# One step of a hybrid decoder layer: dummy products ahead of the small ones, weight parts in another order, and a few moved steps

## The chip, the cores and the metric

The kernel runs on one core of one Trainium2 chip, in one launch. The metric is the device time of that launch in microseconds (us). The core has five engines that work side by side, each through its own instructions in a fixed order: PE (TensorE, matrix products; its weight loads are listed apart as PEld), DVE (VectorE), ACT (ScalarE), POOL (GpSimd) and SP (SyncE, which here issues transfers). Products are written to PSUM, everything else lives in SBUF or in the chip's memory.

## The reference, cut to what matters

Eight sampled sequences of 8 tokens and one prompt of 512 tokens go through one layer; the kernel lays all of them side by side as 576 columns, with the channels on the 128 partitions.

```python
u = rmsnorm(h, norm_mix); P = u @ w_in              # 1024 -> z, xbc, dt, and the RWKV columns rw
# group A (Mamba-2 SSD): causal conv(4) + SiLU on xbc, chunked state space recurrence, gate silu(z), grouped RMSNorm
# group B (RWKV-7): u = rw + (prev - rw) * mu; decay, in-context rate, normalised key kk;
#   S_t = S diag(w) - (S kk)(kk*a)^T + v k^T, read with r; norm per head, bonus, gate
h = h + concat(y_ssd, y_rwkv) @ w_out
h = h + (silu(hf @ w_gate) * (hf @ w_up)) @ w_down   # hf = rmsnorm(h, norm_ffn); 1024 -> 2816 -> 1024
h = h + sigmoid(rmsnorm(h, norm_ple) @ w_ple_gate) * (p @ w_ple_proj)
y = rmsnorm(h, norm_final)                           # and the new states
```

## The kernel before, in words

**Dense tiles.** Each product with a weight matrix is made tile by tile: 128 output channels by 576 columns, in PSUM. For precision every float32 operand is split in two: a rounded first part (hi) and the remainder (lo). A weight block of 128x512 (four 128x128 blocks) is transferred into `raw`, ACT rounds it to `whi` (line 195), and POOL and DVE in turn subtract to make `wlo` (line 198, the turn is kept in `flip`). `whi` and `wlo` have two buffers each. `linear` (line 217) then makes, per 128x128 block and per half of 288 columns, three products through `mm3`: whi with x-hi (line 213), whi with x-lo (214), wlo with x-hi (215). So a weight block gives 24 products, and `whi` is used by the 23rd of them, `wlo` by the 24th.

**Order.** The program is written in Python, and a scheduler that knows the dependencies places each instruction in the queue of its engine when the kernel is built. On the chip each engine then works strictly in that order, waiting for what is not ready.

**Stages.** (1) The opening: x is loaded, an unnormalised split copy `xu` feeds the first tiles (the two low-rank tiles and the six of quarter 0), while the normalised X is made (`norm_x`, line 330: one DVE multiplication and one split per 128 channels, eight in all); `gates` makes the eight gate tiles. (2) Four quarters of group B, four heads each. A quarter has `prep` (decays, keys; `by_channel` at line 489 turns per-token norms into per-channel rows by small products with the identity), `start_states` (line 706, 32 small products with the sampled start states), `gram` (line 581: nine 64-token chunks in five PSUM tiles, 72 products of 64x128, line 593, which ACT and DVE read out and POOL masks), `solve` (30 dependent steps on DVE), `combine` (line 661, 64 products of 32x32 and again 64), `chain` (line 719, nine dependent steps with `core`, `prompt_state` and `outp`) and `head_norm` (line 866). Dense tiles of the next quarter, of the convolution and of z are filled in between. (3) Group A (`ssd`). (4) The output projection: `scaled` (line 1292) adds the group A part, in two passes of eight tiles, and `after` (line 1275) prepares the next input. (5) The feed-forward part, 44 and then 8 tiles. (6) The gated per-layer embedding in two column ranges (320 and 256 columns), each with a final norm and eight stores of `yT`, all issued by SP (line 1392).

ACT needs a table load before a function that its present table does not have; square roots (`inv_norm`, `rstd_by_token`) stand among tanh, exp and sigmoid.

Of the kernel before, what the change touches and what calls it, by code (L numbers as in the profile page):

```python
# [16 lines left out]
P = 128  # L17
# [40 lines left out]


CONV_BC = [8, 9, 10, 11]  # L60
CONV_X = [0, 1, 2, 3, 4, 5, 6, 7]
# [13 lines left out]
def hybrid_step(ctx, tc, A):  # L75
# [15 lines left out]
    def act(out, in_, func=AF.Copy, scale=1.0, bias=0.0):  # L91
        S.activation(out, in_, func, bias=bias, scale=scale)  # L92

# [80 lines left out]
    wat = [0]  # L174
    flip = [0]

    def split(src, pool, tags, shape, lo_eng=None, hi=None, lo=None, hi_eng=None, **kw):
# [11 lines left out]
    def wsplit(src, n, hi=None, lo=None):  # L189
        raw = wp.tile([P, 512], F32, tag="raw", name=nm("raw"), bufs=3)  # L190
        nc.sync.dma_start(raw[:, 0:n], src)
        if hi is None:
            hi = wp.tile([P, 512], F32R, tag="whi", name=nm("whi"))
            lo = wp.tile([P, 512], F32R, tag="wlo", name=nm("wlo"))
        act(hi[:, 0:n], raw[:, 0:n])
        flip[0] += 1
        eng = G if flip[0] % 2 else V
        eng.tensor_tensor(lo[:, 0:n], raw[:, 0:n], hi[:, 0:n].bitcast(F32), ALU.subtract)  # L198
        return hi, lo
# [17 lines left out]
    def linear(xs, ps):  # L217
        nk = len(xs)
        for k in range(0, nk, 4):
            b = min(4, nk - k)  # L220
            hi, lo = wload(b)
            for i in range(b):
                xh, xl = xs[k + i]
                mm3(ps, hi[:, i * P:(i + 1) * P], lo[:, i * P:(i + 1) * P], xh, xl, k + i == 0, k + i == nk - 1)

# [19 lines left out]
    nc.sync.dma_start(sst[:], A["s_shift"])  # L245
    sho = se.tile([P, 26, 9], F32, tag="sho", name="sho")

    def cx_ps():
# [178 lines left out]

    norm_x(3)
    ugh = gate_in()
    norm_x(5)  # L430

# [57 lines left out]
    def by_channel(rn, jj, psum, tag):  # L489

        rnv = rn[:].rearrange("p (w h) -> p w h", w=5)[:, :, jj * 2:jj * 2 + 2].unsqueeze(3)
        if tag:
            rx = sp.tile([P, 5, 2, 64], F32, tag=tag, name=nm(tag), bufs=1)
            V.tensor_copy(rx[:], rnv.to_broadcast([P, 5, 2, 64]))
            rx4 = rx[:, 4]
        else:
            rx = slot("rx", [P, 4, 2, 64])
            V.tensor_copy(rx[:], rnv[:, 0:4].to_broadcast([P, 4, 2, 64]))
            rx4 = s2.tile([P, 2, 64], F32, tag="rx4", name=nm("rx4"))
            V.tensor_copy(rx4[:], rnv[:, 4].to_broadcast([P, 2, 64]))  # L500
        ps = psum()
        for w, a in enumerate(WIN[:4]):
            T.transpose(ps[:, a:a + P], rx[:, w].rearrange("p a b -> p (a b)"), ident[:])
        yield 0, 448, ps[:, 0:448]
        ps = psum()
        T.transpose(ps[:, 0:P], rx4.rearrange("p a b -> p (a b)"), ident[:])
        yield 448, NT, ps[:, 0:P]
# [73 lines left out]
    def gram(s):  # L581

        s.Lst = s2.tile([P, 9, 2, 64], F32, tag="Lst", name=nm("Lst"))
        for gs in ((0,), (1, 2), (3, 4), (5, 6), (7, 8)):
            n = len(gs)
            gl = slice(gs[0], gs[0] + n)
            mk = dgmask if gs[0] == 0 else gmask
            ps = lin.tile([P, 1024], F32, tag="lin", name=nm("lin"))
            for i, g in enumerate(gs):
                for jj in jj2:  # L590
# [70 lines left out]
    def combine(s):  # L661
# [3 lines left out]
        for e in range(2):  # L665
            for z in range(2):
# [4 lines left out]
                              s.Ad[e].rearrange("g s t -> s g t"))  # L671
        Wp = cx_ps()
        Wv = Wp[:].rearrange("p (g j t) -> p g j t", g=8, j=2)
        for g in range(1, 9):
# [5 lines left out]
        for e in range(2):  # L680
# [3 lines left out]
            else:  # L684
                V.tensor_scalar(AA[hi_:hi_ + 32, 1:9], Wv[hi_:hi_ + 32], -1.0, None, ALU.mult)
        Xp = cx_ps()
        Xv = Xp[:].rearrange("p (g j t) -> p g j t", g=8, j=2)
        for g in range(1, 9):
# [30 lines left out]
    def chain(s):  # L719
# [45 lines left out]
        def core(g):  # L765
# [21 lines left out]
        def outp(g):  # L787
            sv = suv(g)
            ow = outs[g]
            for jj in jj2:  # L790
                for e in range(2):
                    T.matmul(ow[H[e], jj], sv[:, jj, 1, e], Gt[:, g, jj, 1, e], start=False, stop=True,  # L792
                             skip_group_check=True)
            act(AR[:, :, g], ow)

# [70 lines left out]
    def head_norm(s, ahead=()):  # L866
# [18 lines left out]
        for jj in jj2:  # L885
# [10 lines left out]
            else:  # L896
                YR.append(split(y, xp, ("xhi", "xlo"), [P, NT], lo_eng=G))

# [5 lines left out]
    for s in Q:  # L904
        if s.q == 0:
            fill(2)
            gates(ugh)
        fill_for(s)
# [443 lines left out]
    for a, b in ((0, 320), (320, NT)):  # L1352
        n = b - a
        acc = None
        for c in range(8):
# [15 lines left out]
            V.tensor_tensor(t, ps, rs[:, a:b], ALU.mult)  # L1371
            act(t, t, AF.Sigmoid)
            V.tensor_tensor(t, t, PL[c][:, a:b], ALU.mult)  # L1373
# [11 lines left out]
        for c in range(8):  # L1385
# [4 lines left out]
            else:  # L1390
                V.scalar_tensor_tensor(h, h, par("norm_final", c), ps, ALU.mult, ALU.mult)
            nc.sync.dma_start(A["yT"][c, :, a:b], h)

# [131 lines left out]
```

## Time and profile before

| what | value |
|---|---|
| median of 3 runs | 1366.8 us (1364.27 to 1370.2) |
| the profiled execution's own time | 1370.43 us |
| its span, first to last instruction | 1368.7 us |
| PE busy | 1259.1 us, 10565 products |
| DVE, ACT, POOL busy | 719.6, 577.4, 550.2 us |
| mean granted TensorE clock | 0.947 of full speed |
| transfers | 135.56 MB, mean 99 GB/s |

Busy times are sums over one engine's instructions; a busy PE is not PE at its peak, since products overlap and their ends are modelled. The granted clock is the share of full speed that PE was given in a stretch. In a row of the timeline stand the start, the duration, the engine, the line, the operation, output and inputs, and in brackets how long the engine had been idle and whose result it waited for.

### The profile page before, as it was taken

To read this page: it belongs to the slowest core of one execution; us is meant where nothing else is said; L and a number is where in the kernel's file an instruction comes from. 1 tells how busy PE (TensorE), PEld (TensorE's weight loads), DVE (VectorE), ACT (ScalarE), POOL (GpSimd) and SP (SyncE) were. 2 spreads that over 40 slices of the span, in tenths; PEclk is the share of its full clock that TensorE was granted. 3 is DMA by queue.
4 is the path that set the end of the run, shared out by engine and by line. 5 is a ranking of instruction groups with operands and counts; after the bars stand their busy time and mean duration, and the time that the engine had idled before them with its cause. 6 is when DMAs were issued, how large, how long until landed. Compare 5 with 4: busy or idle time off the path is not lost.

```text
span 1368.7 us, 26325 instructions
## 1 busy us (share of the span) xinstructions
PE 1259.1 (92%) x10565; PEld 1160.4 (85%) x10565; DVE 719.6 (53%) x1333; ACT 577.4 (42%) x1148; POOL 550.2 (40%) x543
## 2 busy tenths in 40 slices
PE   6897999999989979899989979999999999999986
PEld 5786897789868857777779769999999999999985
DVE  7648766787687785843367676522222221111255
ACT  6565345634653553344425364432332332222253
POOL 5326414632454153133456676432332332334332
PEclk9997899899979989989999989999999999999998
DMA  4322342234223312362644532233232222222432
GB/s 162 124 70 62 85 119 60 81 100 128 61 90 91 101 58 84 88 209 82 189 145 142 183 97 71 70 85 79 84 85 81 83 85 77 82 80 79 148 92 69
DMA packets 94458, 135.56 MB, mean 99 GB/s; under 512 B 34704, under 2 KB 39056, under 8 KB 94336
## 3 DMA queue, kind: packets, MB, share of 16 engines
q1 hardware_dynamic: 94336, 133.88, 32.8%
q8 instruction: 83, 1.36, 0.4%
q14 instruction: 39, 0.32, 0.1%
HBM read 106.10 MB, written 27.75 MB: 98 GB/s over the span
## 4 chain that ended last, share of the span: by engine, by line
PE 60%; DVE 15%; ACT 5%; DMA 5%; issue 4%; POOL 3%; DVEq 0%; SPq 0%; ACTq 0%; POOLq 0%
PE lin L215 16%; PE lin L213 16%; PE lin L214 16%; DVE h L375 2%; DVE Tt L656 1%; DVE tmp L654 1%; DMA raw<-wts 1%; POOL wlo L198 1%; DVE suv L809 1%; PE cx L777 1%; PE lin L593 1%; PE cx L769 1%; DVE wlo L198 1%; PE cx L792 1%; DVE pg L1373 1%
## 5 line engine op out<-in xcount | busy, mean ns | idle before, releaser
L213 PE MATMUL lin<-xhi,whi 128*128 128x288 f32 (+1 forms) x1488 | 450.8, 303 | 3.3 <-ACT whi L92 2.2
L215 PE MATMUL lin<-xhi,wlo 128*128 128x288 f32 (+1 forms) x1488 | 447.9, 301 | 3.2 <-POOL wlo L198 2.2
L214 PE MATMUL lin<-xlo,whi 128*128 128x288 f32 (+1 forms) x1488 | 447.7, 301 | 1.0 <-POOL xlo L186 1.0
L198 POOL TENSOR_TENSOR wlo<-raw,whi 128x512 fp32r<-128x512 f32 x136 | 182.8, 1344 | 501.9 <-ACT whi L92 462.1
L92 ACT ACTIVATE whi<-raw 128x512 fp32r<-128x512 f32 (+1 forms) x272 | 168.8, 621 | 397.7 <-PE lin L214 341.1
L213 PEld LDWEIGHTS lin<-xhi,whi 128*128 128x128 f32 (+1 forms) x1488 | 281.4, 189 | 10.5 <-ACT whi L92 2.6
L215 PEld LDWEIGHTS lin<-xhi,wlo 128*128 128x128 f32 (+1 forms) x1488 | 282.3, 190 | 7.0 <-POOL wlo L198 2.8
L214 PEld LDWEIGHTS lin<-xlo,whi 128*128 128x128 f32 (+1 forms) x1488 | 281.9, 189 | 6.1 <-POOL xlo L186 2.1
L198 DVE TENSOR_TENSOR wlo<-raw,whi 128x512 fp32r<-128x512 f32 (+1 forms) x136 | 98.4, 724 | 167.4 <-ACT whi L92 164.8
L215 PE MATMUL lin<-ah,wlo 128*128 128x288 f32 x352 | 105.0, 298 | 0.9
L213 PE MATMUL lin<-ah,whi 128*128 128x288 f32 x352 | 104.0, 296 | 0.0
L214 PE MATMUL lin<-al,whi 128*128 128x288 f32 x352 | 103.8, 295 | 0.0
L215 PEld LDWEIGHTS lin<-ah,wlo 128*128 128x128 f32 x352 | 66.2, 188 | 3.2 <-POOL wlo L198 2.6
L214 PEld LDWEIGHTS lin<-al,whi 128*128 128x128 f32 x352 | 66.1, 188 | 0.0
L213 PEld LDWEIGHTS lin<-ah,whi 128*128 128x128 f32 x352 | 66.0, 187 | 0.0
L1332 DVE TENSOR_TENSOR sg<-lin,sg 128x576 f32<-128x576 f32 x22 | 16.7, 758 | 82.9 <-PE lin L215 81.7
L1327 DVE TENSOR_TENSOR sg<-lin,rstd 128x576 f32<-128x576 f32 x22 | 16.7, 758 | 69.3 <-PE lin L215 69.0
L654 DVE TENSOR_TENSOR tmp<-L,Tt 72x30 f32<-72x30 f32 (+14 forms) x120 | 48.9, 407 | 3.2
L656 DVE TENSOR_TENSOR Tt<-Tt,tmp 72x30 f32<-72x30 f32 (+14 forms) x120 | 46.1, 384 | 3.4
L213 PE MATMUL lin<-xu,whi 128*128 128x288 f32 x128 | 39.9, 313 | 8.5 <-ACT xu L92 6.9
L215 PE MATMUL lin<-xu,wlo 128*128 128x288 f32 x128 | 40.0, 314 | 7.3 <-DVE wlo L198 5.5
L186 POOL TENSOR_TENSOR al<-sg,ah 128x576 fp32r<-128x576 f32 x22 | 31.5, 1433 | 32.1 <-ACT ah L92 32.1
(370 smaller groups left out, 2513.6 us busy)
## 6 DMA issues: line engine op xcount, KB each, us to landing
raw<-wts SPq DMA_DIRECT2D x271, 256.0 KB, 2.6
S<-s_wkv SPq DMA_DIRECT2D x8, 512.0 KB, 5.1
hd<-s_ssm SPq DMA_DIRECT2D x8, 512.0 KB, 4.0
o_ssm_s<-hd SPq DMA_DIRECT2D x8, 512.0 KB, 2.9
xbc_d<-E SPq DMA_DIRECT2D x12, 288.0 KB, 2.1
x<-xT SPq DMA_DIRECT2D x8, 288.0 KB
gate_d<-g SPq DMA_DIRECT2D x8, 288.0 KB, 2.6
bv_d<-rw SPq DMA_DIRECT2D x8, 288.0 KB
```

What stands on the lines that cost most here:

```text
L92: S.activation(out, in_, func, bias=bias, scale=scale)
L186: eng.tensor_tensor(lo[:], src, hi[:].bitcast(F32), ALU.subtract)
L198: eng.tensor_tensor(lo[:, 0:n], raw[:, 0:n], hi[:, 0:n].bitcast(F32), ALU.subtract)
L213: T.matmul(ps[:, a:b], whi, xhi[:, a:b], start=first, stop=False)
L214: T.matmul(ps[:, a:b], whi, xlo[:, a:b], start=False, stop=False)
L215: T.matmul(ps[:, a:b], wlo, xhi[:, a:b], start=False, stop=last)
L375: V.scalar_tensor_tensor(h[:], E[:, i:i + 600], w(i), h[:], ALU.mult, ALU.add)
L593: T.matmul(ps[:, c:c + 128].rearrange("p (a t) -> p a t", a=2), s.BK[jj][H[e], g].rearrange("p a t -> p (a t)"), s.G[H[e], g, jj, :, e], s ...
L654: V.tensor_tensor(o, L[:, jx:jx + 1, jx + 1:32].to_broadcast([NB, jx, n]), Tt[:, 0:jx, jx:jx + 1].to_broadcast([NB, jx, n]), ALU.mult)
L656: V.tensor_tensor(Tt[:, 0:jx, jx + 1:32], Tt[:, 0:jx, jx + 1:32], o, ALU.subtract)
L1327: V.tensor_tensor(s_[:], ps, rs[:], ALU.mult)
L1332: V.tensor_tensor(s_[:], up, s_[:], ALU.mult)
```

## The change

Every text line below is from the difference of the two programs; the helper functions around it are the same.

- **Beats.** `beat` issues products of a constant mask with a broadcast column, 512 columns wide, into a PSUM tile that the following products overwrite. Their results are used by nothing. They stand ahead of the small products of `by_channel`, `gram` (numbers by the table `BEATS`), `combine`, `start_states` and two steps of one `chain`: 107 in all, 99 of 512 columns and 8 of 256.
- **First weight parts first.** `linear` makes the 16 products with `whi` of a weight block first, and the 8 with `wlo` after them.
- **Inputs one per tile.** `norm_x` is called for one input tile at a time between the first tiles, and `gates` moves behind the third tile of quarter 0.
- **Splits.** In `scaled` and the tiles of that stage DVE alone makes `wlo` (`only`); the last quarter's two outputs are split by DVE and not by POOL.
- **Square root tables.** `root_ready` puts a one-column square root on ACT behind a given instruction: after the last step of the last chain, and after the last sigmoid.
- **Stores.** In the second column range the stores of odd `c` are issued by ACT.

```diff
+BEATS = [(10, 2), (3, 1), (3, 1), (3, 1)]
...
+    def root_ready(ins):
+
+        with tc.issue_after(ins.ins):
+            t = cp.tile([P, 1], F32, tag="rr", name=nm("rr"), bufs=2)
+            act(t[:], eps_t[:, 2:3], AF.Sqrt)
...
-        eng = G if flip[0] % 2 else V
+        eng = only[0] or (G if flip[0] % 2 else V)
...
             hi, lo = wload(b)
+            w = [slice(i * P, i * P + P) for i in range(b)]
             for i in range(b):
-                xh, xl = xs[k + i]
-                mm3(ps, hi[:, i * P:(i + 1) * P], lo[:, i * P:(i + 1) * P], xh, xl, k + i == 0, k + i == nk - 1)
+                for c, d in HV:
+                    T.matmul(ps[:, c:d], hi[:, w[i]], xs[k + i][0][:, c:d], start=k + i == 0, stop=False)
+                    T.matmul(ps[:, c:d], hi[:, w[i]], xs[k + i][1][:, c:d], start=False, stop=False)
+            for i in range(b):
+                for c, d in HV:
+                    T.matmul(ps[:, c:d], lo[:, w[i]], xs[k + i][0][:, c:d], start=False, stop=k + i == nk - 1)
...
+    def beat(ps, n=1, w=512):
+
+        for _ in range(n):
+            T.matmul(ps[:, 0:w], gmask[:].rearrange("p a b -> p (a b)"), gmask[:, 0, 0:1].to_broadcast([P, w]),
+                     start=True, stop=True)
...
-    norm_x(3)
+    norm_x(1)
     ugh = gate_in()
-    norm_x(5)
+    norm_x(1)
...
         ps = psum()
+        beat(ps, 1)
         for w, a in enumerate(WIN[:4]):
...
             ps = lin.tile([P, 1024], F32, tag="lin", name=nm("lin"))
+            beat(ps, BEATS[s.q][bool(gs[0])])
...
         Wp = cx_ps()
+        beat(Wp, 2)
...
         Xp = cx_ps()
+        beat(Xp, 2)
...
+        beat(Zp, 2)
         for jj in jj2:
+            if jj:
+                beat(Zp[:, 256:512], 2, 256)
...
+            if q == 2 and g > 6:
+                beat(ups, 2)
...
+            out = act(AR[:, :, g], ow)
+            if q == 3 and g == 8:
+                root_ready(out)
...
-                YR.append(split(y, xp, ("xhi", "xlo"), [P, NT], lo_eng=G))
+                YR.append(split(y, xp, ("xhi", "xlo"), [P, NT], lo_eng=V))
...
-        if s.q == 0:
-            fill(2)
-            gates(ugh)
+        for i in range(6) if s.q == 0 else ():
+            fill(1)
+            norm_x(1)
+            if i == 2:
+                gates(ugh)
...
+    only[0] = V
     for c in range(8):
         scaled(c, 0)
...
+    only[0] = None
...
+            sig = act(t, t, AF.Sigmoid)
+            if a and c == 7:
+                root_ready(sig)
...
-            nc.sync.dma_start(A["yT"][c, :, a:b], h)
+            (nc.scalar if a and c % 2 else nc.sync).dma_start(A["yT"][c, :, a:b], h)
```

Three places show what the builder made of it. The first is the ACT queue in `prep` of quarter 0, around the square root of the key norms (`rn`). `whi_1159` before and `whi_1161` now is the rounding of the next dense tile's first weight block; `lo`, `pb`, `suv` and `G` are steps of the quarter, `E` and `h` of a convolution tile. Before:

```order
L92 ACTIVATE rn_1097<-cb_990 128x20
L92 ACT_TABLE_LOAD
L92 ACTIVATE lo_1118<-lin_1111,hw 128x576
L92 ACTIVATE pb_1121<-lo_1108 128x576
L92 ACTIVATE suv_1669<-tr_1666 64x4x64 x2
L92 ACTIVATE suv_1663<-tr_1666 64x4x64 x2
L92 ACTIVATE lo_1108<-lo_1108 128x576
L92 ACTIVATE G_982<-ar_981 64x9x64 x2
L92 ACTIVATE whi_1159<-raw_1157 128x512
L92 ACTIVATE E_1079<-lin_1015 128x512
```

The same place in the changed kernel:

```order
L93 ACTIVATE rn_1097<-cb_990 128x20
L93 ACTIVATE whi_1161<-raw_1159 128x512
L93 ACTIVATE E_1079<-lin_1015 128x512
L93 ACTIVATE E_1079<-lin_1015 128x8x8
L93 ACT_TABLE_LOAD
L93 ACTIVATE lo_1118<-lin_1111,hw 128x576
L93 ACTIVATE h_1087<-E_1079,hw 128x600
L93 ACTIVATE pb_1121<-lo_1108 128x576
L93 ACTIVATE suv_1699<-tr_1696 64x4x64 x2
```

The rounding of the weight block stood behind eight other ACT instructions and a table load, and now stands right behind the square root.

The second is PE in `gram` of quarter 1, at the third of its five PSUM tiles (`lin_3149` before, `lin_3195` now; `G` and `bk` are the gram's operands, the `cx` rows are steps of quarter 0's chain). Before:

```order
L777 MATMUL cx_1865<-xs_1862,TT_465 64x64 x4
L782 MATMUL cx_1870<-ar_981,suv_1834 64x64 x4
L593 MATMUL lin_3149<-G_2686,bk_2849 128x128 x2
L593 MATMUL lin_3149<-G_2686,bk_2986 128x128 x2
L593 MATMUL lin_3149<-G_2686,bk_2849 128x128 x2
L593 MATMUL lin_3149<-G_2686,bk_2986 128x128 x2
L792 MATMUL cx_1870<-G_982,suv_1834 64x64
```

In the changed kernel:

```order
L806 MATMUL cx_1895<-xs_1892,TT_435 64x64 x4
L811 MATMUL cx_1900<-ar_981,suv_1864 64x64 x4
L264 LDWEIGHTS gmask
L264 MATMUL lin_3195<-gmask 128x512
L615 MATMUL lin_3195<-G_2720,bk_2885 128x128 x2
L615 MATMUL lin_3195<-G_2720,bk_3024 128x128 x2
L615 MATMUL lin_3195<-G_2720,bk_2885 128x128 x2
L615 MATMUL lin_3195<-G_2720,bk_3024 128x128 x2
L821 MATMUL cx_1900<-G_982,suv_1864 64x64
```

One beat stands ahead of the tile's products; the products and the chain's steps around them keep their places.

The third is DVE in the opening, behind the normalisation of the last input tile (`x_220`). `rw` is the token shift of the two low-rank tiles, `xlo` the remainders of the normalised inputs, `wlo_573` before and `wlo_518` now is the remainder of a weight block. Before:

```order
L332 SCALAR_TENSOR_TENSOR x_220<-x_220,pv,rstd_263 128x576
L348 SCALAR_TENSOR_TENSOR rw_337<-sst,pv,rw_337 128x9
L349 SCALAR_TENSOR_TENSOR rw_337<-u_335,pv,rw_337 128x511
L351 SCALAR_TENSOR_TENSOR rw_337<-u_335,pv,rw_337 128x8x7
L186 TENSOR_TENSOR xlo_351<-x_200,xhi_350 128x576
L186 TENSOR_TENSOR xlo_361<-x_204,xhi_360 128x576
L348 SCALAR_TENSOR_TENSOR rw_427<-sst,pv,rw_427 128x9
L349 SCALAR_TENSOR_TENSOR rw_427<-u_425,pv,rw_427 128x511
L351 SCALAR_TENSOR_TENSOR rw_427<-u_425,pv,rw_427 128x8x7
L186 TENSOR_TENSOR xlo_442<-x_206,xhi_441 128x576
L186 TENSOR_TENSOR xlo_452<-x_216,xhi_451 128x576
L198 TENSOR_TENSOR wlo_573<-raw_570,whi_572 128x512
```

In the changed kernel:

```order
L351 SCALAR_TENSOR_TENSOR x_220<-x_220,pv,rstd_263 128x576
L367 SCALAR_TENSOR_TENSOR rw_337<-sst,pv,rw_337 128x9
L368 SCALAR_TENSOR_TENSOR rw_337<-u_335,pv,rw_337 128x511
L370 SCALAR_TENSOR_TENSOR rw_337<-u_335,pv,rw_337 128x8x7
L194 TENSOR_TENSOR xlo_351<-x_200,xhi_350 128x576
L367 SCALAR_TENSOR_TENSOR rw_417<-sst,pv,rw_417 128x9
L368 SCALAR_TENSOR_TENSOR rw_417<-u_415,pv,rw_417 128x511
L370 SCALAR_TENSOR_TENSOR rw_417<-u_415,pv,rw_417 128x8x7
L194 TENSOR_TENSOR xlo_432<-x_202,xhi_431 128x576
L206 TENSOR_TENSOR wlo_518<-raw_515,whi_517 128x512
```

All eight normalisations still stand ahead of the remainder of the weight block; two of the four `xlo` between them are gone. `wlo_573` belonged to the second weight block of its tile, `wlo_518` belongs to the first of the same tile.

More of the change, by code (lines that the diff above doesn't have):

```diff
@@ L91, in act @@
     def act(out, in_, func=AF.Copy, scale=1.0, bias=0.0):
-        S.activation(out, in_, func, bias=bias, scale=scale)
+        return S.activation(out, in_, func, bias=bias, scale=scale)
+    def root_ready(ins):
+        with tc.issue_after(ins.ins):
+            t = cp.tile([P, 1], F32, tag="rr", name=nm("rr"), bufs=2)
+            act(t[:], eps_t[:, 2:3], AF.Sqrt)
     lins, turn = [lin], [0]
@@ L175, in hybrid_step @@
     flip = [0]
+    only = [None]
     def split(src, pool, tags, shape, lo_eng=None, hi=None, lo=None, hi_eng=None, **kw):
@@ L505, in by_channel @@
         ps = psum()
+        beat(ps, 1)
         T.transpose(ps[:, 0:P], rx4.rearrange("p a b -> p (a b)"), ident[:])
@@ L793, in outp @@
                              skip_group_check=True)
-            act(AR[:, :, g], ow)
+            out = act(AR[:, :, g], ow)
+            if q == 3 and g == 8:
+                root_ready(out)
         def prompt_state(g):
@@ L1371, in hybrid_step @@
             V.tensor_tensor(t, ps, rs[:, a:b], ALU.mult)
-            act(t, t, AF.Sigmoid)
+            sig = act(t, t, AF.Sigmoid)
+            if a and c == 7:
+                root_ready(sig)
             V.tensor_tensor(t, t, PL[c][:, a:b], ALU.mult)
```

## The prediction

> **What bounds the kernel now.** I read the engine shares and the chain of waits on the page, then busy times by stretch. From the page, busy time and share of each engine, and the shares of the chain that ended last:
>
> ```profile
> PE 1259.1 (92%) x10565; PEld 1160.4 (85%) x10565; DVE 719.6 (53%) x1333; ACT 577.4 (42%) x1148; POOL 550.2 (40%) x543
> ...
> PE 60%; DVE 15%; ACT 5%; DMA 5%; issue 4%; POOL 3%; DVEq 0%; SPq 0%; ACTq 0%; POOLq 0%
> ```
>
> PE is busy for 92% but only 60% of the chain is its work; the rest of its busy time lies beside something else that ends later. The windows (stretch, length, busy time and count of PE, PEld, DVE, ACT and POOL, granted clock, DMA share, GB/s) separate the two kinds of stage:
>
> ```profile
> 99.00:697.00 598.00, 540.78 (x5010) 465.25 (x5011) 414.82 (x862) 282.33 (x625) 234.50 (x271) 0.91 0.34 101
> 870.00:1300.00 430.00, 429.05 (x3209) 426.42 (x3208) 93.72 (x134) 128.16 (x202) 143.56 (x106) 1.00 0.31 87
> 386.00:406.00 20.00, 17.04 (x161) 13.87 (x161) 15.60 (x32) 10.66 (x27) 6.21 (x11) 0.50 0.29 97
> 408.00:420.00 12.00, 11.27 (x119) 9.29 (x116) 4.96 (x14) 5.99 (x18) 11.54 (x12) 1.00 0.36 76
> 858.26:864.00 5.74, 5.06 (x24) 4.83 (x25) 5.49 (x4) 1.35 (x2) 4.64 (x3) 0.70 0.32 91
> ```
>
> From 870 to 1300 us, the feed-forward part, PE has no idle time and full clock; nothing in the change touches this, so 430 us stand fixed. From 99 to 697 us, the quarters, PE is busy 90% at a mean clock of 0.91, with DVE at 69%. The change works there and at the edges of stages. What the clock does to a dense product is seen in PE's timeline at a stage's start:
>
> ```profile
> 99.13 0.41 PE L213 MATMUL lin<-xhi,whi 128*128 128x288 f32 x1 [1.69 <-ACT whi L92]
> ...
> 102.20 0.44 PE L215 MATMUL lin<-xhi,wlo 128*128 128x288 f32 x1
> 102.44 0.44 PE L213 MATMUL lin<-xhi,whi 128*128 128x288 f32 x1
> ...
> 103.01 0.30 PE L213 MATMUL lin<-xhi,whi 128*128 128x288 f32 x1
> 103.14 0.30 PE L214 MATMUL lin<-xlo,whi 128*128 128x288 f32 x1
> ...
> 107.11 0.40 PE L215 MATMUL lin<-xhi,wlo 128*128 128x288 f32 x1 [0.82 <-POOL wlo L198]
> ...
> 235.36 0.40 PE L215 MATMUL lin<-xhi,wlo 128*128 128x288 f32 x1 [1.10 <-POOL wlo L198]
> ```
>
> Starts are 0.24 us apart up to 102.4 and 0.13 (0.133 over longer runs) from 103.0: half the clock doubles a dense product. I work against the profiled execution: 1370.43 us, of it 1368.7 span, 3.6 above the median of 1366.8. A result within 0.5% (6.8 us) is no change here, about what a measurement of this kernel can tell, as its runs spread over 0.43%.
>
> **Weight parts first, and the queue of ACT (T1).** The block that PE waits for at 99.13 stood behind this on ACT:
>
> ```profile
> 97.07 1.36 ACT L92 ACTIVATE G<-ar 64x576 f32<-64x576 f32 x2
> 98.45 0.63 ACT L92 ACTIVATE whi<-raw 128x512 fp32r<-128x512 f32 x1
> ```
>
> By the order it now comes eight instructions and a table load earlier, so the gap of 1.69 goes, and with it the slow products behind it: about 15 at 0.24 in place of 0.133, 1.6 us. Within a block, `whi` is now last used by the 16th product instead of the 23rd, so its buffer is free about 7 products (0.93 us) earlier, and `wlo` is first asked for 15 products (at most 2.0 us) later, more than the waits of 0.82 and 1.10 above. Sum 1.69 + 1.6 + 0.82 + 1.10 = 5.2. The number of products doesn't change. DVE's work in these stages (69%) comes next and takes some back; I take −4, ends −5.2 and 0.
>
> **Splits of the output projection on DVE (T2).** ACT, then PE, at the 16th tile of that stage:
>
> ```profile
> 856.34 0.78 ACT L92 ACTIVATE xhi<-h,pv 128x576 fp32r<-128x576 f32 x1 [2.02 <-POOL h L1298]
> ```
>
> ```profile
> 858.26 0.40 PE L213 MATMUL lin<-yh,whi 128*128 128x288 f32 x1 [1.81 <-ACT whi L92]
> ```
>
> ACT waited 2.02 us for POOL, which also makes half of the `wlo`; with those on DVE, POOL's sum comes earlier. Gain: the gap of 1.81 and some 19 of the 24 products up to 864 (the last of the windows) at 0.24 in place of 0.133, 2.0 us, together 3.8. DVE takes four to eight more `wlo`; it was busy 5.49 of 5.74 us just behind the gap, so it may end later instead: one DVE step, up to +1. I take −3.5, ends −3.8 and +1.
>
> **Last quarter's head norm (T3).** ACT's table load ahead of the norm's square root, POOL's split at the end of that norm, and DVE's price for a split of that shape:
>
> ```profile
> 684.85 1.28 ACT L92 ACT_TABLE_LOAD   x1
> 686.15 0.28 ACT L92 ACTIVATE gnr<-tr,eps_t 128x20 f32<-128x20 f32 x1
> ```
>
> ```profile
> 696.40 1.43 POOL L186 TENSOR_TENSOR xlo<-gb,xhi 128x576 fp32r<-128x576 f32 x1 [1.40 <-ACT xhi L92]
> ```
>
> ```profile
> 41.60 1.41 DVE L186 TENSOR_TENSOR xlo<-x,xhi 128x576 fp32r<-128x576 f32 x2
> ```
>
> The load moves ahead of its need (1.28), the split falls from 1.43 to 0.70 (0.73): −2.0 at most, 0 if DVE is late there. I take −2.
>
> **Stores and the last square root (T4).** Stores, last sums, and ACT's last square root:
>
> ```profile
> 1362.49 3.77 SPq L1392 DMA_DIRECT2D yT<-h  x8
> ```
>
> ```profile
> 1361.98 2.44 DVE L1391 SCALAR_TENSOR_TENSOR h<-h,pv,lin 128x256 f32<-128x256 f32 x6 [1.20 <-ACT rs L92]
> ```
>
> ```profile
> 1357.29 1.28 ACT L92 ACT_TABLE_LOAD   x1
> ...
> 1360.33 0.26 ACT L92 ACTIVATE rn<-lin,eps_t 128x2 f32<-128x2 f32 x1 [1.75 <-PE lin L312]
> ```
>
> SP's eight stores take 3.77 us, 0.47 each, and end at 1366.26, while the last sum ends at 1364.42. With two queues the last store can be issued one issue behind that sum, 1364.9: −1.3. ACT's price for such an issue is in no row; at SP's 0.47 ACT's four hide in the sums, at twice that they end no earlier than today, at three times that 1.9 later. The best end is no delay behind the last sum, −1.8. Ends −1.8 and +1.9; I take −1.3, from SP's row. The table load at 1357.29 is already over 1.7 us before its root is due, so that `root_ready` brings nothing: this part does not do what it seems to.
>
> **Normalising one tile at a time (T5).** DVE in the opening, and PE behind it:
>
> ```profile
> 32.79 6.66 DVE L332 SCALAR_TENSOR_TENSOR x<-x,pv,rstd 128x576 f32<-128x576 f32 x5
> ```
>
> ```profile
> 45.99 0.61 PE L215 MATMUL lin<-xu,wlo 128*128 128x288 f32 x1 [5.45 <-DVE wlo L198]
> ```
>
> The code reads as if a tile's `wlo` no longer stood behind the normalisations; the order has all eight still ahead of it. So PE's stall of 5.45 stays. It moves from a tile's second block to its first. There PE can run 16 `whi` products, stops at about 38.7, and gets its `wlo` about 1.4 us earlier (two `xlo` of 0.70 less), at 44.5, but with 32 products left of the tile where at 46.0 there were 22: 10 × 0.24 = 2.4 more, 1.4 less, +1. Ends 0 and +3, the latter if the two left-out `xlo` stall a later tile instead (2 × 0.70). I take +1.
>
> **Beats (T6).** A beat of 512 columns costs 512/288 × 0.133 = 0.236 us at full clock, one of 256 0.118; the 99 and 8 make 24.3 us. The chain's PE work is 0.60 × 1368.7 = 821; less 429 up to 1300 and some 50 of the 69 behind it, about 342 lies in the first 870 us, 39%. So 39% of 24.3, 9.5 us, falls on the path; 14 beats stand where PE idles (four in the opening's stall, ten in the 2.74 below), 1.3 less: +8.
>
> What they may win is the clock. If the rate is full or half, a mean of 0.91 over 598 us is 2 × 0.09 × 598 = 108 us at half rate, of which PE worked 90%: 97 us, 49 saved if all of it ran at full rate. With 39% on the path that is 19; beats stand at many of the places, not at all, and I let them win three quarters: −14. Net −6. The bounds are −49 and +24.3.
>
> Why not more: where the clock is low, other engines are often the pace. Products of the gram, at low and at full clock:
>
> ```profile
> 126.73 1.22 PE L593 MATMUL lin<-G,bk 64*128 64x128 f32 x4 [2.74 <-POOL bk L565]
> ...
> 401.47 2.08 PE L593 MATMUL lin<-G,bk 64*128 64x128 f32 x16
> ...
> 407.42 1.16 PE L593 MATMUL lin<-G,bk 64*128 64x128 f32 x16
> ```
>
> Sixteen take 2.08 at half and 1.16 at full clock, but at 408 to 420 (windows above) POOL was busy 11.54 of 12 us at full clock: there a faster PE only waits. At 386 to 406 the clock was 0.50 for 20 us with PE at 85% and DVE at 78%: there beats can win.
>
> Can filling gaps of this size win the clock at all? In the trace it falls after short ones: 1.69 us before 99.13, 1.81 before 858.26, and products at half rate behind both. [...]
>
> **Sum.** −4 − 3.5 − 2 − 1.3 + 1 − 6 = −15.8 on the profiled execution, 1354.6; from the median, 1351.0.
>
> **The rivals.**
>
> *R1, the clock wins it all.* If PE is what every stage of the quarters waits for, the whole 49 is won and the whole 24.3 paid: −24.7 in place of −6. Sum −34.5, 1332. For it: PE at 90%. Against: POOL's 11.54 of 12 and a chain with 40% on others.
>
> *R2, beats are cost alone.* The granted clock follows something that beats don't change (how full a whole stretch is, say), and they lie on PE where PE is late: +24.3 in place of −6, sum +14.5, 1381, slower. It decides once the beats on the path cost 16.6 us more than they win (6.8 + 9.8, the other terms). For it: 386 to 406 had a clock of 0.50 with PE at 85%, so being busy alone doesn't hold it up. Against: 39% of the chain, not all, is PE's there. [...]
>
> *R3, other engines carry the quarters.* DVE, at 69%, and POOL take back both T1 and T6: what stands is −3.5 − 2 − 1.3 + 1 = −5.8, 1361.0, within 0.5%. For it: the solve's 30 dependent steps on DVE in each quarter. Against: the gaps at 99.13 and 107.11 sit on PE itself with dense work behind.
>
> **How the numbers follow.** Forecast 0.53, R1 0.15, R3 0.20, R2 0.12 (its milder form with net +8 lands at 1365, no change, and is counted to R3). Range: the forecast's own, with T1 to T5 at their good ends together (−12.8) or at the bad ends of all but T4 (+4), and beats between −14 (19 won at a cost of 5) and −2 (10 won at a cost of 8), is 1340 to 1369; it must reach to R1, 1332, nearly in full, and leave out R2: 1333 to 1369. Faster by over 0.5%: R1 and nine tenths of the forecast and some of R3, 0.7. Within: most of R3 and the forecast's slow end, 0.19. Slower: R2, 0.11.
>
> **What would show it.** Right: PE's gap at the first dense tile behind quarter 0's `prep` gone; none over 1 us before a product with `wlo` in the quarters; mean clock of the quarters 0.95 or more; beats' busy time 24 to 40 us; the table load of the last head norm off its square root; last store issue under 2 us behind the last sum; PE's stall in the opening still about 5 us. Wrong: a clock still at 0.91 with the beats in place (R2), a clock near 1.00 with the quarters as long as before and PE idle on DVE or POOL (R3), or the quarters shorter by 40 us (R1). A mean clock that rises only because the beats themselves run at full rate, with dense products still 0.24 apart, would break T6's reason.

## The result, and the profile after

The changed kernel is slower: 1382.7 us (median of 4 runs, 1378.1 to 1387.0) against 1367.8 (4 runs), a ratio of 1.0111 with a 95% interval of 1.0083 to 1.0138. The profiled execution took 1387.03 us, 16.6 more than that of before (each is the slowest of its four); its span is 1385.3.

From the page after, busy times and the chain:

```profile
PE 1288.7 (93%) x10672; PEld 1173.2 (85%) x10672; DVE 727.9 (53%) x1343; ACT 580.6 (42%) x1150; POOL 534.5 (39%) x533
...
PE 66%; DVE 14%; ACT 4%; DMA 4%; issue 2%; POOL 1%; SPq 0%; DVEq 0%; ACTq 0%; POOLq 0%
```

PE is busy 29.6 us longer and idle 13.0 less (1385.3 − 1288.7 = 96.6, before 109.6): together the 16.6 of the span. So other engines hold PE up less than before; PE itself has more to do. The mean granted clock, and the windows over the quarters and over the feed-forward part (columns as in the prediction):

```profile
core 0: 1385.3 us, clock 0.944
```

```profile
98.00:716.00 618.00, 564.70 (x5089) 472.10 (x5088) 407.81 (x863) 286.63 (x628) 228.14 (x273) 0.91 0.32 96
888.00:1317.00 429.00, 427.84 (x3214) 426.84 (x3213) 101.28 (x136) 129.77 (x205) 150.01 (x108) 1.00 0.30 87
```

The quarters went from 598 to 618 us, with the clock at 0.91 as before (from the same dense product on, which starts at 99.13 before and, as shown below, at 95.07 now, it is 598 and 621). Every share on record in the two traces is 0.5 or 1, so the whole execution spent 2 × (1 − 0.944) × 1385.3 = 155 us at half clock, before 2 × 0.053 × 1368.7 = 145: the beats are in place and the time at half clock did not fall. A single execution says this only roughly: among all executions of before the figure runs from 117 to 165 us, with a median of 145.

The first dense tile behind the `prep` of quarter 0. On ACT, the rounding of its first and of its second weight block, and the table load between them:

```profile
93.22 0.63 ACT L93 ACTIVATE whi<-raw 128x512 fp32r<-128x512 f32 x1 [1.21 <-issue]
...
94.95 1.28 ACT L93 ACT_TABLE_LOAD   x1
...
100.40 0.62 ACT L93 ACTIVATE whi<-raw 128x512 fp32r<-128x512 f32 x1
```

On PE, the first products of these two blocks, and of the next tile:

```profile
95.07 0.38 PE L233 MATMUL lin<-xhi,whi 128*128 128x288 f32 x1
...
101.06 0.40 PE L233 MATMUL lin<-xhi,whi 128*128 128x288 f32 x1 [1.30 <-ACT whi L93]
...
109.76 0.61 PE L233 MATMUL lin<-xhi,whi 128*128 128x288 f32 x1 [3.01 <-ACT lo L93]
```

The block for which PE waited 1.69 us before (it is the 493rd dense product in both traces) now starts at 95.07, 4.1 us earlier and without an idle gap. But the wait moved on: ACT's other work now stands ahead of the next block, for which PE waits 1.30 us, and 3.01 us stand behind that, where ACT comes late with `lo`. The opening's stall stands where the prediction put it (it starts at 38.7 and ends at 45.0, forecast 38.7 and 44.5):

```profile
45.01 2.29 PE L237 MATMUL lin<-xu,wlo 128*128 128x288 f32 x8 [6.28 <-DVE wlo L206]
```

These rows show the late moves at work: the square root of the last head norm, whose table load now lies 9 us ahead of it (each of the two traces has 25 such loads, all of 1.28 us, 12 of them right ahead of a square root), the split on DVE in 0.75 in place of POOL's 1.43, and the last stores.

```profile
699.17 1.28 ACT L93 ACT_TABLE_LOAD   x1
...
708.76 0.26 ACT L93 ACTIVATE gnr<-tr,eps_t 128x20 f32<-128x20 f32 x1
...
1380.12 1.95 ACTq L1429 DMA_DIRECT2D yT<-h  x4
```

```profile
716.95 0.75 DVE L194 TENSOR_TENSOR xlo<-gb,xhi 128x576 fp32r<-128x576 f32 x1
...
1379.62 2.04 DVE L1428 SCALAR_TENSOR_TENSOR h<-h,pv,lin 128x256 f32<-128x256 f32 x5
```

ACT issues a store in 0.49 us, nearly as SP did before (0.47); its last issue ends at 1382.07, 0.41 behind the last sum (1381.66), where SP's ended 1.84 behind it.

### The profile page after: what moved, and what is told of

It reads as the page before. It is cut to its first block, busy times and chain, and to the rows that moved or that the text cites. A ratio compares the mean times of both kernels' runs of the same rounds, so it can differ in the third digit from the quotient of the medians.

```text
span 1385.3 us, 26531 instructions
## 1 busy us (share of the span) xinstructions
PE 1288.7 (93%) x10672; PEld 1173.2 (85%) x10672; DVE 727.9 (53%) x1343; ACT 580.6 (42%) x1150; POOL 534.5 (39%) x533
## 4 chain that ended last, share of the span: by engine, by line
PE 66%; DVE 14%; ACT 4%; DMA 4%; issue 2%; POOL 1%; SPq 0%; DVEq 0%; ACTq 0%; POOLq 0%
PE lin L233 16%; PE lin L234 16%; PE lin L237 16%; PE lin L615 2%; DVE Tt L678 2%; DVE tmp L676 1%; DVE h L394 1%; PE cx L796 1%; PE cx L806 1%; DVE wlo L206 1%; PE cx L821 1%; DVE suv L840 1%; DMA L<-Ld 1%; PE lin L1398 1%; PE cx L858 1%
## 5 line engine op out<-in xcount | busy, mean ns | idle before, releaser
L233 PE MATMUL lin<-xhi,whi 128*128 128x288 f32 x1440 | 408.3, 308 | 7.6 <-ACT lo L93 4.0
L234 PE MATMUL lin<-xlo,whi 128*128 128x288 f32 x1440 | 405.4, 304 | 1.9 <-DVE xlo L1312 1.1
L233 PEld LDWEIGHTS lin<-xhi,whi 128*128 128x128 f32 x1440 | 277.5, 193 | 14.5 <-ACT lo L93 4.7
L234 PEld LDWEIGHTS lin<-xlo,whi 128*128 128x128 f32 x1440 | 276.9, 192 | 7.1 <-issue 1.7
L237 PE MATMUL lin<-xhi,wlo 128*128 128x288 f32 x1440 | 234.2, 301 | 0.0
L237 PEld LDWEIGHTS lin<-xhi,wlo 128*128 128x128 f32 x1440 | 205.5, 191 | 3.8 <-issue 2.1
L206 DVE TENSOR_TENSOR wlo<-raw,whi 128x512 fp32r<-128x512 f32 x144 | 102.6, 713 | 142.2 <-PE lin L237 100.5
L237 PE MATMUL lin<-ah,wlo 128*128 128x288 f32 x352 | 54.8, 296 | 0.0
L237 PEld LDWEIGHTS lin<-ah,wlo 128*128 128x128 f32 x352 | 49.3, 188 | 0.0
L615 PEld LDWEIGHTS lin<-G,bk 64*128 64x128 f32 x288 | 30.2, 248 | 17.2 <-issue 9.2
```

Source lines behind the costliest of these rows:

```text
L233: T.matmul(ps[:, c:d], hi[:, w[i]], xs[k + i][0][:, c:d], start=k + i == 0, stop=False)
L234: T.matmul(ps[:, c:d], hi[:, w[i]], xs[k + i][1][:, c:d], start=False, stop=False)
L237: T.matmul(ps[:, c:d], lo[:, w[i]], xs[k + i][0][:, c:d], start=False, stop=k + i == nk - 1)
L615: T.matmul(ps[:, c:c + 128].rearrange("p (a t) -> p a t", a=2), s.BK[jj][H[e], g].rearrange("p a t -> p (a t)"), s.G[H[e], g, jj, :, e], s ...
```

## The experiments

Each kernel was timed over five rounds beside the kernel before. "Half clock" is 2 × (1 − clock) × span of the profiled execution, as above (before 145, changed 155). "Moved" counts how many of the 2,050 small products stand more than 24 dense products away from where they stood in the kernel before, from the two orders of instructions.

The main theory at the start (B): the beats lie on PE's path and win no clock. The rivals: the new order of weight parts lost the time (O), or the beats won and something else lost more (C).

**e1, the changed kernel without beats.**

```diff
-        for _ in range(n):
+        for _ in range(0):
```

> The changed kernel with all 107 beats left out, everything else kept. Theory B (the beats are cost on PE's path and win no clock): 24 us less than the changed kernel, about 1359, ratio to before 0.993, mean clock of the quarters still near 0.91. Theory O (the new order of weight parts and of what the builder places around it is what lost the time): no more than 5 us less, 1378 to 1383, ratio 1.008 or more. Theory C (the forecast: beats win more clock than they cost, something else lost more): slower than the changed kernel, 1385 to 1390, with more time at half clock.

Measured: 1372.6 us, ratio 1.0056 (1.0035 to 1.0077). By the ratios the beats cost 0.55%, 7.5 us, not 24, and without them the kernel is still slower than before. Half clock is 172 us (clock 0.937, span 1368.8), 17 more than with beats (19 by the medians of all executions, 171 and 152): they do win clock, some 8.6 us of PE's time, and cost more. None of the three theories is right as it stood.

**e2, the changed kernel with the old order of parts in `linear`; e3, the kernel before with the new order alone.** The edit of e3 is the hunk of `linear` in the change, that of e2 its reverse.

> The changed kernel with the old order of weight parts (the three products of a 128x128 block together). Theory B: 2 to 5 us more than the changed kernel, 1385 to 1388, ratio 1.013 to 1.015. Theory O: 12 to 20 us less, 1363 to 1371, ratio near 1.000.

> The kernel before with the new order of weight parts alone. Theory B: 0 to 5 us faster than before, ratio 0.996 to 1.000. Theory O: 10 to 20 us slower, ratio 1.007 to 1.015.

Measured: e2 1.0111 (1.0081 to 1.0140), no different from the changed kernel, with only 124 us at half clock; e3 1.0078 (1.0055 to 1.0101), 10.6 us slower than before. The same edit costs 10.6 us in one company and nothing in another; costs don't add. The profile of e3 says by what it is slower:

```profile
core 0: 1375.2 us, clock 0.937
```

Its PE is busy 1268.3 us, 9.2 more than before with the same number of products; half clock is 173 us, 28 more than before. e3's `moved` is 225.

**e4, the kernel before with the 107 beats alone.**

> The kernel before with the 107 beats alone. Theory B: 20 to 25 us slower, ratio 1.015 to 1.018, mean clock of the quarters within 0.01 of 0.91. Theory O: within 5 us of before. Theory C: 6 us faster, ratio 0.996, clock 0.95.

Measured: 1.0149 (1.0123 to 1.0176), 20 us slower, as B said. Half clock is 150 us (by the medians of all executions 136, against 150 for the kernel before beside it), and 174 small products are moved: the builder places the beats like other products and sets the rest around them.

**e5, the new order of parts from the feed-forward part on.**

```diff
+            if hf[0]:
...
+                continue
...
+    hf[0] = True
     mix2.close()
```

> The kernel before with the new order of weight parts only from the feed-forward part on; the order of everything ahead of it is the same as before. Theory S (the new order saves the short waits of the eight down tiles, 144.2 us before and 140.0 us in all three kernels that had it, and loses its time in the quarters, where the builder places the small work another way): 4 us faster than before, ratio 0.997. Theory P (the new order itself is slower wherever it stands): 0 to 4 us slower, ratio 1.000 to 1.003.

Measured: 1362.2 us, 0.9964 (0.9946 to 0.9982), 4.7 us faster: theory S. The gain is in the eight down tiles. The first and last products with `whi` there, before and in e3:

```profile
1150.33 0.30 PE L213 MATMUL lin<-ah,whi 128*128 128x288 f32 x1
...
1294.55 0.29 PE L213 MATMUL lin<-ah,whi 128*128 128x288 f32 x1
```

```profile
1162.13 0.29 PE L225 MATMUL lin<-ah,whi 128*128 128x288 f32 x1
...
1302.13 0.30 PE L225 MATMUL lin<-ah,whi 128*128 128x288 f32 x1
```

144.2 us against 140.0; up to the very last product of the stage, a `wlo` one, it is 144.5 against 140.7, 3.8 us. What went is, for the most part, this wait, once per tile, which no row marks as idle (starts 0.43 and then 0.24 apart, in place of 0.13):

```profile
1168.06 0.29 PE L214 MATMUL lin<-al,whi 128*128 128x288 f32 x1
1168.49 0.40 PE L215 MATMUL lin<-ah,wlo 128*128 128x288 f32 x1
1168.73 0.30 PE L213 MATMUL lin<-ah,whi 128*128 128x288 f32 x1
```

So the new order is not slow in itself; here, where nothing small lies between dense products, it wins.

**e6, the moves alone (no beats, old order of parts); e7, e6 with e5's edit.**

> The changed kernel without beats and with the old order of weight parts: only the inputs one per tile, the splits on DVE, the square root tables and the stores on two queues. If the parts add up: 3 to 5 us faster than before, ratio 0.996 to 0.998 (0.9 us less than that would say that the tail's and the output projection's gains are lost in the opening). If the moves need the other parts: ratio 1.000 or more.

> The moves of the kernel above and the new order of weight parts from the feed-forward part on. Theory S: the sum of both, 7 to 9 us faster than before, ratio 0.994. Theory P: 0 to 5 us faster, ratio 0.997 to 1.000.

Measured: e6 1.0059 (1.0043 to 1.0076), 8 us slower where 3 to 5 faster was expected: a miss. e7 1.0032 (1.0014 to 1.0051), better than e6 by nearly e5's gain, and also a miss of both theories. If the rest of the moves win what was forecast, one of them costs over 10 us.

**e8, the changed kernel with beats 32 columns wide.**

```diff
     def beat(ps, n=1, w=512):
+        w = 32
```

> The changed kernel with all beats 32 columns wide in place of 512 or 256 (the builder moves some of the small work, since it knows their size). Theory W (PE's time is the path in the quarters, a beat costs its columns, and the clock follows the columns streamed in a window of 3.41 us): close to the kernel without beats, 1370 to 1376, half-clock time 165 to 180 us. Theory I (a beat costs as an instruction, by its weight load and its wait for a PSUM tile, and the clock follows whether PE is idle): close to the changed kernel, 1378 to 1385, half-clock time about 155 us.

Measured: 1.0099 (1.0073 to 1.0125), 1379.9 us, as theory I had it, but with 176 us at half clock, as W had it. Ten beats of 32 columns are over 0.41 us after the first one's start, ten of 512 columns 2.35 us (a row of e8, then of the changed kernel):

```profile
120.19 0.41 PE L264 MATMUL lin<-gmask 128*128 128x32 bf16 x10
```

```profile
119.76 2.35 PE L264 MATMUL lin<-gmask 128*128 128x512 bf16 x10
```

The narrow ones start 0.026 us apart, (0.41 − 0.18) / 9 with 0.18 the duration of one alone, so 107 are worth some 3 us, yet the kernel is 0.43%, 6 us, slower than without beats. It has 182 small products more than 24 dense ones away from where e1 has them. That suggests that a part of what beats cost is the order that the builder makes around them; what their weight loads and their waits for a PSUM tile add was not separated from it. The kernel with wide beats is only 0.12% slower, which is within the noise; that it has less time at half clock (155 us against 176) fits wide beats winning most of their columns back as clock.

**e9, the moves without those of the opening; e10, e9 with e5's edit; e11, the opening's move alone.** The edits are the hunks of the change, kept or left out.

> The kernel before with the moves of the changed kernel except those of the opening: splits on DVE, square root tables, stores on two queues. The order on PE is that of before up to the end of the last quarter. Theory L (the opening's move is what cost 8 us, since it shifts the order of the small products in all quarters; the late moves save what was forecast): 4 to 7 us faster than before, ratio 0.995 to 0.997. Theory M (the late moves cost it): 3 to 8 us slower, ratio 1.002 to 1.006.

> The late moves of the kernel above and the new order of weight parts from the feed-forward part on, where it had saved 4.7 us alone. Theory L: 9 to 12 us faster than before, ratio 0.991 to 0.993, and faster than both kernels of the case. Theory M: 0 to 5 us slower.

> The kernel before with the inputs normalized one per tile and the gates moved, nothing else. Theory L: 10 to 14 us slower than before, ratio 1.007 to 1.010, of which at most 3 us stand in the opening itself and the rest in the quarters, with 15 to 30 us more at half clock. Theory M: within 3 us of before.

Measured: e9 0.9961 (0.9938 to 0.9983), 5 us faster, about the −6.8 that the prediction gave these parts. Of T2, the largest of them, its trace shows the wait of 1.81 us and the window at half clock behind it gone; a wait of 1.04 us for DVE's `wlo` is left in that stage. e10 0.9932 (0.9907 to 0.9956), 1355.4 us: it is faster than both kernels of the case. e11 1.0126 (1.0090 to 1.0162), 17 us slower. Theory L holds for the opening alone.

**e12, 24 more beats in the longest stretch at half clock.**

```diff
-BEATS = [(10, 2), (3, 1), (3, 1), (3, 1)]
+BEATS = [(10, 2), (3, 1), (3, 1), (3, 3)]
...
             for b in range(8):
+                if s.q == 3:
+                    beat(Zp[:, 256:512], 1, 256)
```

> The changed kernel with 16 more beats of 256 columns between the start state products of the last quarter and 8 more of 512 in its gram; the order on PE ahead of them is the same. They cost 3.8 us at full clock. Theory W (the clock of the next 3.41 us follows the columns streamed in this one, full from about 2800 on): the stretch of 24 us at half clock there shrinks to 10 us or less, and the whole is between 3 us faster and 3 us slower than the changed kernel. Theory I (the clock follows whether PE is idle; it has hardly any idle time there already): the stretch stays at half clock and the whole is 4 to 8 us slower.

Measured: 1.0194 (1.0164 to 1.0225), 0.83% or 11 us slower than the changed kernel, which is past what theory I said. The stretch in the changed kernel and in e12:

```profile
520.85:544.75 23.90, 23.54 (x200) 18.89 (x196) 8.93 (x25) 6.59 (x20) 6.12 (x10) 0.50 0.07 24
```

```profile
515.75:543.00 27.25, 26.40 (x205) 19.65 (x208) 7.41 (x22) 5.88 (x18) 6.54 (x9) 0.50 0.11 40
```

PE is busy 98% and 97% of these windows, at half clock throughout. So in these two stretches the clock didn't follow the idle time that the profile shows. What PE did in one of them, in the changed kernel:

```profile
531.36 0.40 PE L741 MATMUL cb<-G,S 64*64 64x16 f32 x4
531.69 0.61 PE L264 MATMUL cb<-gmask 128*128 128x256 bf16 x2
532.23 1.25 PE L741 MATMUL cb<-G,S 64*64 64x16 f32 x18
533.41 0.69 PE L767 MATMUL tr<-ident,rw 128*128 128x128 f32 x2
```

22 × 16 + 2 × 256 + 2 × 128 = 1,120 columns in 2.7 us, where dense products at full clock stream 288 in 0.133, 5,800 in the same time. e12 added beats, but of the eight windows of 3.41 us that stood at half clock there (from 515.63 on, each product counted where it starts) seven held 1,760 to 2,304 columns, and only the last, with 3,008, was followed by full clock; 22 of this trace's products have no record, so that the counts are a little low. My estimate of how many beats it takes was wrong. The counts over all such windows stand at the end.

**e13, the changed kernel with the old opening; e14, e13 without beats.** These and the next two were run because the parts cost 17, 20 and 10.6 us alone and 15 together.

> The changed kernel with the old opening (three and five inputs normalized at once, the gates behind the second tile); 220 of 8866 products on PE stand elsewhere. Theory A (the opening costs in the changed kernel what it cost alone, 17 us): 1363 to 1369, ratio 1.000 or less. Theory D (the opening costs through the order that the builder then makes of the quarters, and that order is another one here): within 5 us of the changed kernel, ratio 1.007 to 1.015, and the cost is that of the beats and of the first weight parts in the quarters.

> The kernel above without the beats: the new order of weight parts everywhere and the late moves. Theory A and D both: the first weight parts' 10.6 us less the late moves' 5, ratio 1.003 to 1.005, so that the beats stand at 10 to 20 us under D and under 0 under A.

Measured: e13 1.0117 (1.0095 to 1.0140), e14 1.0045 (1.0028 to 1.0061): theory D. In the changed kernel the opening costs nothing; there no small product is moved by it past more than six dense ones. Beats cost 10 us (e14 to e13), and the first weight parts 11.5 (e9 to e14).

With these runs two of the parts can be crossed. All four kernels have the late moves and no beats:

| ratio to before | old order of weight parts | new order |
|---|---|---|
| old opening | 0.9961 (e9) | 1.0045 (e14) |
| new opening | 1.0059 (e6) | 1.0056 (e1) |

Either edit alone costs 0.8 to 1.0%, and the second one then costs next to nothing (0.1% at most, within the noise). So what a part costs depends on what is there already, and a sum by parts, in whatever order, prices the order in which they are added as well. Beats cost in all four pairs on record: 7.5 us (e1 to the changed kernel), 7 (e6 to e2), 10 (e14 to e13) and 20 (before to e4), although in each pair they shorten the time at half clock, by 19, 39, 25 and 14 us (medians over all executions).

**e15, only the gates later (`fill(3)` for `fill(2)`); e16, only the inputs one per tile.**

> The kernel before with the gates behind the third tile of quarter 0 in place of the second; 96 products on PE move, all in the opening. Theory D: within 3 us of before, since the quarters keep their order. Theory G (the gates' place is what costs): 8 us slower or more.

> The kernel before with one input normalized per tile, the gates where they were; on PE nothing moves in the opening, the first move stands in quarter 1, 1080 products in all. Theory D: 10 to 17 us slower than before, nearly all of it behind the first 200 us. Theory G: within 3 us of before.

Measured: e15 0.9999 (0.9988 to 1.0011); e16 1.0097 (1.0075 to 1.0118). e16 moves nothing on PE in the opening: in the traces PE's first difference stands at 238 us, in quarter 1, and 43 small products are moved far. The loss stands in quarters 2 and 3; that stretch, and a place in it, before and in e16:

```profile
481.20:611.30 130.10, 111.00 (x1167) 93.16 (x1160) 88.86 (x199) 55.92 (x128) 42.01 (x48) 0.86 0.36 111
559.00:572.00 13.00, 8.82 (x75) 6.15 (x75) 11.64 (x32) 3.52 (x9) 2.69 (x3) 0.74 0.22 69
```

```profile
479.30:620.70 141.40, 120.93 (x1175) 100.74 (x1174) 89.94 (x201) 56.45 (x127) 41.71 (x48) 0.80 0.32 102
563.50:580.50 17.00, 11.71 (x92) 8.47 (x92) 12.27 (x36) 2.30 (x8) 1.05 (x3) 0.57 0.35 85
```

The same work takes 11.3 us longer, PE is busy 9.9 longer with nearly the same products, and the clock is 0.80 for 0.86. This is not the scatter of single executions: from the 1,993rd to the 2,289th dense product, which lies in this stretch, the five traces with the old opening and the old order ahead of the feed-forward part (before, e5, e9, e10, and e15, which moves the gates alone) take 88.9 to 90.4 us, and the four with the new opening (e6, e7, e11, e16) 98.3 to 99.0. One place of it, PE before:

```profile
566.99 0.69 PE L801 MATMUL cx<-suv,bkt 128*64 128x64 f32 x8
567.47 0.64 PE L792 MATMUL cx<-G,suv 128*64 128x64 f32 x6
568.48 1.80 PE L879 MATMUL cx<-ar,cen 128*128 128x288 f32 x3 [0.37 <-ACT ar L92]
```

and in e16:

```profile
568.08 0.69 PE L801 MATMUL cx<-suv,bkt 128*64 128x64 f32 x8
568.56 0.64 PE L792 MATMUL cx<-G,suv 128*64 128x64 f32 x6
569.77 1.31 PE L769 MATMUL cx<-suv,G 128*128 128x128 f32 x4 [0.57 <-DVE suv L809]
```

Before, wide products of 288 columns follow the chain's step and the clock is full again from 570.5; in e16 the chain's next step follows, with narrow products, and it stays at half. The edit also shifts the order on DVE, ACT and POOL in the quarters, and no run separates that from the order on PE.

**e17, e10 with a milder new order ahead of the feed-forward part** (per 128x128 block four products with the first part, then two with the second).

> The fastest kernel so far (late moves, first weight parts first from the feed-forward part on, 0.68% faster than before) with the tiles ahead of the feed-forward part changed to a milder form of the new order: per 128x128 block four products with the first part and then two with the second. The number of products is the same; the builder moves 45 of 2050 small products past more than 24 dense ones. Theory D (what costs is where the builder then puts the small products in the quarters): 8 to 20 us slower than that kernel, ratio to before 0.999 to 1.008. Theory F (what costs is the second parts' standing together behind four blocks): within 4 us of that kernel, ratio 0.990 to 0.996.

Measured: 0.9982 (0.9969 to 0.9994), 1363.1 us: 0.5% slower than e10, between what both theories gave. The order still costs, less than in e3. How much of e3's cost is the places of the small products and how much the parts' own order stays open, since the builder can't be made to keep the one and change the other. No kernel tried it with the same places.

## Why the prediction was wrong, step by step

The sum by the experiments, each added to the one before: late moves −0.39% (e9), first weight parts +0.84% (e14), beats +0.72% (e13), opening −0.06% (the changed kernel): +1.11%. In another order the same total splits otherwise: late moves −0.39% (e9), opening +0.98% (e6), beats +0.52% (e2), first weight parts 0.00%. The beats and the late moves keep their signs in both; the opening and the weight parts share one cost.

- **Beats (T6: −6; measured +7 to +10 beside the other parts, +20 alone).** The step that failed is "let them win three quarters: −14". Of the 49 us of PE's time that the clock could give, three quarters would be 37; in the finished kernel the beats take 17 us from the time at half clock (172 to 155), about 8.6 of PE's time, and in no pair more than 20 (e6 to e2, by medians). The price of a beat at full clock was right (0.22 us by its rows, 0.236 forecast; all 107 are busy 37.0 us), but "39% of 24.3 falls on the path" was too little: alone they cost 20 (e4). That the chain's share of PE, an average, is too low just at the small products, where PE at half clock is itself the slow engine, is my reading of the window of 23.9 us above (PE busy 23.54). By e8 part of the cost may be order, not PE time.
- **Weight parts first (T1: −4; measured +11 with the old opening, 0 with the new one).** "The gap of 1.69 goes" came true for that block and failed for PE: ACT's work was reordered, not lessened, and it held PE for 1.30 and 3.01 us at the next places. And "nothing in the change touches" the feed-forward part failed the other way: there the order wins 3.8 us, from waits that the idle list doesn't show. Where the parts cost, they come with more half clock (e3: 28 us), which no term of mine held.
- **Opening (T5: +1; 0 in the changed kernel, 17 alone).** The stall came where and as it was worked out. That I looked for its cost in the opening only was wrong for e11 and e16: most of it arose over 400 us later, in an order that an edit in the opening had shifted.
- **Late moves (T2 to T4: −6.8; e9 measured −5.3).** Right in mechanism and nearly in size: the wait of 1.81 gone, table load off the chain, split at 0.75, last store issue 0.41 behind the last sum.
- **The term that the sum put at nothing.** What I had in no term and no rival is that each edit rearranges the quarters: I priced every part in the order of before. e16 shows what that can cost: nothing on PE changes in the opening, 43 small products are moved far, 13 us lost, while e15, which moves none far, loses nothing. How many are moved says little about how much it costs (225 in e3 for 10.6 us), and by which products or engines it costs stays open.
- **The rivals.** R2 had the sign. Its mechanism came true only in part: half clock goes with thinly filled stretches (by the counts at the end, 159 of 165 windows with fewer than 2,000 columns were followed by it), but beats changed the time at half clock, by 14 to 39 us in the four pairs. Its milder form, the +8 of T6 with no clock won, is near what the beats cost beside the other parts (7 to 10 us), but there they did win clock. That its time, 1381, is close to the measured 1382.7 is luck: its 24.3 for the beats is too much by 14 or more, and it took T1 at −4. Its reason against itself, "39% of the chain", was the weak one.

## What to carry to other kernels

Where a builder sets the order, an edit need not stay local: compare the whole order first, see what moved far from where it was, and expect a time from that alone that can outweigh the edit. Try parts of a change one at a time and then together, and expect that the costs don't add; here what was worth having (the late moves, and the new order of parts in the feed-forward part: e10, 0.68% faster) was hidden under what was not. Filling PE with dummy work won clock here (14 to 39 us less at half clock in the four pairs) and still cost 7 to 20 us in each; no run found a place where it pays.

## What the runs showed of the hardware that was not expected

The clock changed on a grid: in the first six kernels profiled (before, the changed one, e1 to e4), stretches at half clock last 3.4, 6.8, 10.2, 13.7, 17.1, 20.5 or 23.9 us, multiples of 3.41 (the last one, which the kernel's end cuts off, aside). The traces hold no share but 0.5 and 1, and the grid lies 0.41, 2.02, 1.29, 0.85, 0.69 and 0.70 us behind the first instruction in these six. A window, here, is one step of this grid. What went with the share in the next window is how many columns PE streamed in this one. Counted from the six traces up to 1300 us, where the clock is on record: of 165 windows with fewer than 2,000 columns 159 were followed by half clock, of 1,925 with 3,200 or more 9, of the 170 between them 79 (in the traces of before and of the changed kernel alone 51 of 54, 3 of 641 and 26 of 55). At 0.133 us a dense product, a window holds some 7,400. How busy PE is by its rows told less: of 25 windows that it was busy for 95% or more with fewer than 2,000 columns, 23 were followed by half clock. So PE ran at half clock while it was busy nearly without a gap on narrow products (23.54 of the 23.90 us of the stretch above), and a gap of 1.69 us was followed by half clock where the rest of its window was thin (the window that holds it, 95.99 to 99.40 before, has PE busy for 0.94 us and 832 columns). That the count of columns is the cause, and not something that goes with it, was not tested by a run that changes it alone; e12, which tried, stayed at 2,304 or fewer in all windows of its stretch but the last.
